# The low halves of the feed-forward output weights by an accumulating DMA instead of a subtraction on VectorE

## The chip, the cores and the metric

The kernel runs on one core of one Trainium2 chip. The metric is the device time of one execution in microseconds; the time before is the median of three runs, 1916.57 us (1915.85 to 1919.64). A profile of one further execution, taken by the hardware profiler, stands behind every row that is shown here.

## The reference

512 tokens of width 1024 go through two transformer blocks, all in float32. The first block has block-sparse attention and differential attention side by side, merged by gates, and a feed-forward; the second has a half-weighted feed-forward, two mixers, a cross attention to a memory and another half-weighted feed-forward. The three feed-forwards are alike, and the change lies in their last product alone:

```python
D_FF = -(-8 * D_MODEL // (3 * 256)) * 256          # 2816
f = (jax.nn.silu(h @ w_gate[l]) * (h @ w_up[l])) @ w_down[l]      # block 1

def swiglu(h, w_gu, w_down):                                      # block 2, twice
    gu = h @ w_gu
    gate, up = jnp.split(gu, 2, axis=-1)
    return (jax.nn.silu(gate) * up) @ w_down
```

## The kernel before

**Halves.** Every float32 operand of a large product is kept as two tiles of a shorter format (`F32R`): a high half, the rounded value, and a low half, the rest. One product is three matmuls (`mm3`: L371 high by high, L372 high weight or activation by the other's low, L373 low by high), summed in PSUM. The weights come as float32 from memory and are halved on the chip by `split` (L399 to L403): ScalarE copies the raw tile into the high half, which rounds it (L402), then VectorE subtracts the high half from the raw tile (L403).

**Weights' way.** `wpieces` streams a weight matrix in pieces of 128 x 1024 values (512 KB). SyncE issues one load for each (L263); two pieces share a raw slab `wr`, and there are two slabs. The halves go to tiles `wh` and `wl`, four buffers each. So a load waits until both pieces of the slab's last content have been halved, and a cast waits until TensorE has done with the `wh` that stood in its buffer four pieces earlier.

**Feed-forward.** The 22 k tiles of the inner width (2816 = 22 x 128) are done in groups: four k tiles each, the last one six. For a group TensorE makes the gate and up products (most of them by Winograd's seven products, for which VectorE also forms sums of the raw weights, L305 to L308), ScalarE the silu (L1264), VectorE the product of both (L1272), and `split` the halves `q` of the result. The output product of one group (`wide_steps` over `w_down`, L1286) is run in shares between the next group's gate and up products, by the generator `between`. It has two column parts of 512; a piece of `w_down` is two k tiles by 512 columns, so a feed-forward has 22 pieces of it, 16 within the loop and six behind it, of the last group. The last group's second part goes token tile by token tile (`by_token`), so that the norm that follows can begin with the first one. Only then are all its three pieces needed at once.

**Order.** Each engine runs its own instructions in the order that a scheduler gave them when the program was built; weights' loads and halvings have a higher priority (`WPRIO`). Engines wait for each other by semaphores. SyncE's queue carries all loads, among them `x_rows(x_d)` (L195), which in the last part of the first feed-forward brings back eight tiles of the residual stream that were spilled earlier to memory from GpSimd's queue (L554).

**Names.** In the rows below `b<-wh,q` is a `w_down` product of a weight's high half and an activation's half, `b<-wl,q` one with the low half; `a<-...` and `b<-w,...` are gate and up products. Buffers' numbers are left out in the profile, and stand behind the names in the order of instructions.

Of the kernel before, what the change touches and what calls it, by code (L numbers as in the profile page):

```python
# [14 lines left out]
AF = mybir.ActivationFunctionType  # L15
ALU = mybir.AluOpType
AX = mybir.AxisListType

P = 128
# [58 lines left out]
def STEP(pe=0.0, dve=0.0, act=0.0, ops=(), lat=0.0, free=0, need=0, back=0):  # L78
    """A part of a chain or of a product as weave sees it: time on the tensor engine; then on the vector engine and
    on the scalar engine, or on these and GpSimd (D, A, G) in turns; the least delay to the next part; banks freed and needed; how  # L80
    many parts back the next one's inputs lie."""
    return Step(pe, dve, act, ops, lat, free, need, back)
# [11 lines left out]
def transformer_blocks_kernel(  # L94
# [93 lines left out]
    def x_rows(src, get=None):  # L188
        """Token-major tiles: [t, u] holds tokens 128 t.. and columns 512 u.. ."""
        res = {}  # L190
        for t in range(4):
            for u in range(2):
                tl = (get or wt)()
                tc.keep_in_program_order(
                    nc.sync.dma_start(tl, src[t * P:(t + 1) * P, u * 512:(u + 1) * 512]))  # L195
                res[t, u] = tl
        return res
# [67 lines left out]

    def wslab(src, kt, cols, later=None):
        return list(wpieces(src, kt, cols, later))

    def wpieces(src, kt, cols, later=None):
        """Streams src ([kt*128, cols]) in pieces (k, n, high, low) of n k tiles from k on."""  # L270
        per = max(1, 1024 // cols)
        for k in range(0, kt, per):
            n = min(per, kt - k)
            if k % (2 * per) == 0:
                whole = raw_slab()
            raw = whole[:, k % (2 * per) * cols:][:, :n * cols]
            wload(raw, src, k, n, cols)
            hi, lo = [t[:, :n * cols] for t in halves_w()]
            halve = lambda hi=hi, lo=lo, raw=raw: split(hi, lo, raw)
            if later is None or k == 0:  # L280
                with tc.high_priority(WPRIO):
                    halve()
            else:
                later.append(halve)
            yield k, n, hi.rearrange("p (k c) -> p k c", c=cols), lo.rearrange("p (k c) -> p k c", c=cols)

    def sums_w(src):
        """Winograd's seven sums of a 256-column slab's quarters [k tile of a pair][half of the columns], in halves."""
# [23 lines left out]
    def sums_x(act, get):  # L312
        """The operand's side of it: per product the halves of its sum, pair of k tiles by pair."""
# [25 lines left out]
    def slab_sums(ws, xs):  # L339
        """A 256-column slab by Winograd's seven products: tiles of the first 256 tokens' first 128 columns and the others'  # L340
        second ones, and of the others' first and the first's second ones."""
# [33 lines left out]
    def slab_feat(slab, kt, act, bank=None):  # L375
        """Two 128-column outputs of a 256-column slab, features on partitions, one after the other."""
# [9 lines left out]
    def slab_tok(slab, kt, act, ntt, cols):  # L386
        """Token-major outputs of a slab, token tile by token tile."""
# [11 lines left out]
    def split(hi, lo, src, scale=None):  # L399
        """hi + lo = src * scale."""  # L400
# [14 lines left out]
    def in_order(chain):  # L415
        """Keeps what the blocks of one chain trace in this order on its engines."""
# [25 lines left out]
    def rms_col(sums, eps):  # L442
        """(sum of sums + eps) ** -0.5 per token."""
# [7 lines left out]
    def squares(f):  # L451
        """Per token the sum of squares over D."""
# [4 lines left out]
    class PreNorm:  # L457
        """Token-major rows -> feature-major operand: rows * rstd, transposed, times the gain, in halves."""
# [17 lines left out]
        def operand(self, src, *before):  # L476
            """The operand and, as its parts come, its product with the 256 columns of src; before that, other products."""
# [38 lines left out]
    class PostNorm:  # L516
        """x += rmsnorm(f) * g, by tokens, and on to the next norm."""
# [10 lines left out]
        def add(self, t, c0, f, fg, eng):  # L528
            """Takes columns c0.. of f; fg = f * gain."""
# [4 lines left out]
        def row(self, t):  # L534
            """In two stages, for others' work between them."""
# [36 lines left out]
    # distances s - t and the masks are kept negated: the logits are formed negated, so that their  # L572
    # minimum is at once the exponent's bias
# [19 lines left out]
    def stack_q(ps, scale, tag):  # L593
        """Of two heads' 64 features: per head [high; low], or the other way round, on 128 partitions."""
# [5 lines left out]
    def stack_k(ps, tag):  # L600
        """Of two heads' 64 features: per head [high; high] and [low; low] on 128 partitions."""
# [9 lines left out]
    def qk(ps, lh, rh):  # L611
        """All four terms of a head's product, one of its operands [high; low], the other twofold."""
# [5 lines left out]
    def softmax_rows(pt, bias, ps, su):  # L618
        """pt = exp(max - (bias + ps)) of the negated logits, su its row sums."""
# [23 lines left out]
    def fill_ready(accs, consume, dve, act, lat=0.0):  # L643
        """Products made with the norm."""
# [18 lines left out]
    def weave(chains, fills, width, banks, model):  # L663
        """Emits dependent chains, and independent products between their parts, as one order of the tensor engine.

        The parts of a chain that are not yet due, by what they cost each engine, leave room for a product.
        """
# [7 lines left out]
        def place(engine, t, d):  # L675
            """The end of d on an engine, in the first gap from t on."""
# [27 lines left out]
        def start(c):  # L704
            """When a chain's next part can start."""
# [42 lines left out]
    def flip(jobs):  # L748
        """Transposes [128 q, 128 keys] blocks side by side; returns their halves."""
# [43 lines left out]
    def p_flips(blocks, dst):  # L793
        """Transposed probability blocks [i, j], by key tiles: 0 with queries 0.., 1 with 128.., 2 and 3."""
# [20 lines left out]
    def fold(dst, ps, hh):  # L815
        """The two halves' sum on the head's partitions."""
# [4 lines left out]
    def moba_open(p_):  # L821
        """What the two heads of a pair share: the choice of blocks."""
# [78 lines left out]
    def diff_head(hd):  # L901
        """The first softmax is left unnormalised; its row sums come back with the norm."""
# [67 lines left out]
    # gated merge  # L970
# [108 lines left out]
    def mem_slabs(slabs):  # L1079
        """Products for the keys (0 - 3) and the values (4 - 7) of the memory's heads."""  # L1080
# [22 lines left out]
    def wide_steps(src, kt, act, emit, parts, early=True, begun=None, held=0):  # L1103
        """Token-major product: emit(tok tile, c0, psum) for the column parts (c0, cols, by_token).

        An emit in stages has the next token tile's first stage before its last. The first part may have been
        begun, with the first k tiles held in its accumulators.
        """
# [16 lines left out]
        for c0, cols, by_token in parts:  # L1125
            k0 = held if c0 == 0 else 0
            slab = ((k + k0, n, hi, lo) for k, n, hi, lo in wpieces(src[k0 * P:, c0:c0 + cols], kt - k0, cols))
# [86 lines left out]
    def pools(first, second, mid):  # L1214
        """Where the operand's sums lie, half of them in one place, and the middle's halves."""
# [3 lines left out]
    def ffn(wg, wu, wd, add, emit, groups, sums, rest, mid):  # L1219
        """sums: the slabs whose products take Winograd's form."""  # L1220
# [11 lines left out]
        def quarters(ts, wino, to_wino):  # L1232
            """Winograd's two tiles (wino) or those of 128 columns each: how the other form's, or the same, lie in them."""
# [6 lines left out]
        def by_tokens(pairs, wino):  # L1240
            """The two k tiles' halves, token tile by token tile."""
# [6 lines left out]
        for gi, (a, b) in enumerate(groups):  # L1248
# [3 lines left out]
            def between():  # L1252
                """A share of the last group's output product, between the slabs."""
# [32 lines left out]
            before = wide_steps(wd[a * P:b * P], n, mids, fn, ((0, 512, False), (512, 512, b == NF)), False)  # L1286
# [51 lines left out]
    def rstd_rows(sq, ones):  # L1338
        """(mean of squares of a token's head + 1e-6) ** -0.5, on every feature's partition."""
# [12 lines left out]
    def sigmoid(dst, src):  # L1352
        """exp(min(x, 0) - log(1 + exp(-|x|)))."""
# [6 lines left out]
    def hgrn_chain(hd):  # L1360
# [15 lines left out]
        def decayed(e, hl):  # L1376
            """e holds exponents; turned into key (lower) and query (upper) operands."""
# [22 lines left out]
        # the weights of key tile j with the queries from 128 j on, in halves  # L1400
# [113 lines left out]
    def sb_head(pair, hh):  # L1514
        """Stick-breaking attention, queries on partitions: with sp = log(1 + exp(z)) a key's weight is
        exp(z - the sum of sp from it to the last key before the query)."""
# [235 lines left out]
    def fill_mo():  # L1752
        """Half of the columns of the output product, as far as the first heads go; its accumulators stay open."""
# [75 lines left out]
```

## Time and profile before

| | |
|---|---|
| median of three runs | 1916.57 us |
| profiled execution, first to last instruction | 1918.7 us |
| TensorE's granted clock, mean | 0.995 of full speed |
| TensorE busy | 1885.0 us (98%) |
| VectorE busy | 1387.3 us (72%) |
| ScalarE busy | 929.8 us (48%) |
| GpSimd busy | 176.4 us (9%) |
| subtractions of weights' low halves, all weights | 381 of 1217 ns, 462.7 us |
| casts of weights' high halves, all weights | 381 of 1036 ns, 393.7 us |

The profile gives each engine's busy time over the span, cut into rows by line, engine, operation and tiles. A busy share is a mean over stages that differ, so the stages are cut out by windows in time. In a timeline each row is one instruction, or several alike in a row, with its start and duration; a bracket at its end tells how long the engine had been idle before it and what ended that. A chain of waits, followed back from the last instruction, tells which engine's work stood on the path that set the end.

### The profile page before, as it was taken

What the parts mean: (1) busy time and instruction counts of PE and PEld (TensorE: products, weight loads), DVE (VectorE), ACT (ScalarE), POOL (GpSimd) and SP (SyncE); (2) the same over time, 40 slices, a digit from 0 to 9 for tenths busy, and PEclk for the clock granted to TensorE, in tenths of its full rate; (3) what the DMA queues carried; (4) which work ended last, traced back from release to release, by engine and by line L of the source; (5) the groups of instructions that cost most, each with busy time, mean ns of one, the idle gap of its engine ahead of it and who ended that gap; (6) DMA issues with size and microseconds to landing.
All of it is one profiled execution on the core that took longest, in us unless ns stands there. A gap on an engine that the chain in (4) does not pass through costs nothing.

```text
span 1918.7 us, 29315 instructions
## 1 busy us (share of the span) xinstructions
PE 1885.0 (98%) x11566; PEld 1690.5 (88%) x11566; DVE 1387.3 (72%) x2217; ACT 929.8 (48%) x1537; POOL 176.4 (9%) x272
## 2 busy tenths in 40 slices
PE   8999999999999999999999999999999999999998
PEld 7899888888999998889999988888988778999997
DVE  6777635468778786677878757878886448878785
ACT  5666534364534345443344456657555344434443
POOL 2340100050000002000000010330420000000000
PEclk9999999999999999999999999999999999999999
DMA  5221223462232324423232342211223222332322
GB/s 180 67 67 56 78 66 132 143 203 88 89 111 90 122 91 163 150 88 111 88 111 88 110 159 88 66 45 39 90 93 110 77 75 84 106 110 89 111 88 88
DMA packets 161452, 192.40 MB, mean 100 GB/s; under 512 B 7361, under 2 KB 131362, under 8 KB 161314
## 3 DMA queue, kind: packets, MB, share of 16 engines
q1 hardware_dynamic: 159746, 185.80, 29.2%
q0 software_dynamic: 1280, 4.20, 0.6%
q8 instruction: 91, 1.49, 0.3%
q10 hardware_dynamic: 288, 0.52, 0.1%
q14 instruction: 47, 0.39, 0.1%
HBM read 182.11 MB, written 8.39 MB: 99 GB/s over the span
## 4 chain that ended last, share of the span: by engine, by line
PE 86%; issue 5%; DVE 4%; ACT 2%; POOL 1%; POOLq 0%; ACTq 0%; DVEq 0%
PE b L372 16%; PE b L373 16%; PE b L371 16%; PE a L371 10%; PE a L372 10%; PE a L373 10%; PE a L513 4%; PE b L615 1%; PE b L489 1%; DVE wl L403 1%; PE b L753 1%; PE b L1444 1%; DVE w L1540 1%; ACT wh L402 1%; PE b L883 0%
## 5 line engine op out<-in xcount | busy, mean ns | idle before, releaser
L403 DVE TENSOR_TENSOR wl<-wr,wh 128x1024 fp32r<-128x1024 f32 (+1 forms) x381 | 462.7, 1217 | 270.6 <-ACT wh L402 261.6
L402 ACT CAST wh<-wr 128x1024 fp32r<-128x1024 f32 (+1 forms) x381 | 393.7, 1036 | 439.0 <-PE b L372 152.3
L371 PE MATMUL b<-wh,q 128*128 128x512 f32 x672 | 262.4, 390 | 0.0
L372 PE MATMUL b<-wl,q 128*128 128x512 f32 x672 | 262.0, 390 | 0.0
L373 PE MATMUL b<-wh,q 128*128 128x512 f32 x664 | 258.5, 389 | 0.0
L371 PE MATMUL a<-h,wh 128*128 128x512 f32 (+1 forms) x660 | 238.2, 361 | 0.0
L373 PE MATMUL a<-h,wl 128*128 128x512 f32 (+1 forms) x660 | 234.9, 356 | 0.0
L372 PE MATMUL a<-h,wh 128*128 128x512 f32 (+1 forms) x660 | 234.7, 356 | 0.0
L372 PE MATMUL b<-h,wh 128*128 128x256 f32 (+1 forms) x568 | 175.9, 310 | 0.0
L371 PE MATMUL b<-h,wh 128*128 128x256 f32 (+1 forms) x568 | 175.9, 310 | 0.0
L373 PE MATMUL b<-h,wl 128*128 128x256 f32 (+1 forms) x568 | 175.9, 310 | 0.0
L371 PEld LDWEIGHTS b<-wh,q 128*128 128x128 f32 x672 | 126.3, 188 | 24.8
L373 PEld LDWEIGHTS b<-wh,q 128*128 128x128 f32 x664 | 124.7, 188 | 26.4
L372 PEld LDWEIGHTS b<-wl,q 128*128 128x128 f32 x672 | 126.3, 188 | 24.3
L372 PE MATMUL a<-s,wh 128*128 128x256 f32 (+1 forms) x488 | 141.2, 289 | 0.0
L373 PEld LDWEIGHTS a<-h,wl 128*128 128x128 f32 x660 | 124.6, 189 | 18.3
L371 PEld LDWEIGHTS a<-h,wh 128*128 128x128 f32 x660 | 124.7, 189 | 18.0 <-issue 0.5
L372 PEld LDWEIGHTS a<-h,wh 128*128 128x128 f32 x660 | 124.8, 189 | 17.9 <-issue 0.5
L372 PEld LDWEIGHTS b<-h,wh 128*128 128x128 f32 x568 | 108.3, 191 | 5.6
L373 PEld LDWEIGHTS b<-h,wl 128*128 128x128 f32 x568 | 108.2, 191 | 5.6
L371 PEld LDWEIGHTS b<-h,wh 128*128 128x128 f32 x568 | 108.1, 190 | 5.6
L372 PEld LDWEIGHTS a<-s,wh 128*128 128x128 f32 x488 | 93.1, 191 | 1.2
(374 smaller groups left out, 4201.9 us busy)
## 6 DMA issues: line engine op xcount, KB each, us to landing
wr<-in_ffn_w_gu_dram SPq DMA_DIRECT2D x88, 512.0 KB
wr<-in_w_in_dram SPq DMA_DIRECT2D x68, 512.0 KB
wr<-in_ffn_w_down_dram SPq DMA_DIRECT2D x44, 512.0 KB
wr<-in_w_gate_dram SPq DMA_DIRECT2D x22, 512.0 KB
wr<-in_w_up_dram SPq DMA_DIRECT2D x22, 512.0 KB
wr<-in_w_down_dram SPq DMA_DIRECT2D x22, 512.0 KB
wr<-in_mem_w_kv_dram SPq DMA_DIRECT2D x16, 512.0 KB
wr<-in_w_out_dram SPq DMA_DIRECT2D x10, 512.0 KB
```

The costliest lines, as they stand in the source:

```text
L371: T.matmul(ps, lh, rh, start=first, stop=False)
L372: T.matmul(ps, lh, rl, start=False, stop=False)
L373: T.matmul(ps, ll, rh, start=False, stop=last)
L402: A.copy(hi, src)
L403: V.tensor_tensor(lo, src, f32(hi), op=ALU.subtract)
L489: T.transpose(banks[k][:, t * P:(t + 1) * P], self.s[t, k // 4][:, (k % 4) * P:(k % 4 + 1) * P], ident)
L513: T.matmul(accs[m], lh, rh, start=c == 0 and n in (0, 2), stop=c == KT - 1 and n > 3)
L615: T.matmul(ps, lh[n], rh[n], start=n == 0, stop=n == 1)
L753: T.transpose(ps[:, o * P:(o + 1) * P], blk, ident)
L1444: T.matmul(ps[:, gg * 64:(gg + 1) * 64], e[:, gg * P:(gg + 1) * P], up, start=True, stop=True)
L1540: V.tensor_tensor_scan(out=back, data0=ones_c.to_broadcast([P, sl.stop - sl.start]), data1=back, initial=0.0, op0=ALU.mult, op1=ALU.add)
```

## The change

`wpieces` and `wide_steps` get a parameter `halver`, and the feed-forwards hand `split_added` to the output product's `wide_steps`. It makes the low half of a piece in another way: ScalarE writes the negated, rounded raw tile into the low half, and an accumulating DMA from GpSimd's queue adds the raw tile to it, from SBUF to SBUF. As the rounding of −x is minus the rounding of x, the sum is the same low half. All 66 pieces of `w_down` (22 in each of three feed-forwards) go this way; all other weights, among them the gate and up weights, stay with `split`. The rest of the diff blanks comments and docstrings, and moves line numbers by some lines.

```diff
+    def split_added(hi, lo, src):
+        A.copy(hi, src)
+        A.activation(lo, src, AF.Copy, scale=-1.0)
+        nc.gpsimd.dma_start(lo, src, accum_op=ALU.add)
...
-    def wpieces(src, kt, cols, later=None):
+    def wpieces(src, kt, cols, later=None, halver=None):
...
-            halve = lambda hi=hi, lo=lo, raw=raw: split(hi, lo, raw)
+            halve = lambda hi=hi, lo=lo, raw=raw: (halver or split)(hi, lo, raw)
...
-    def wide_steps(src, kt, act, emit, parts, early=True, begun=None, held=0):
+    def wide_steps(src, kt, act, emit, parts, early=True, begun=None, held=0, halver=None):
...
-            slab = ((k + k0, n, hi, lo) for k, n, hi, lo in wpieces(src[k0 * P:, c0:c0 + cols], kt - k0, cols))
+            slab = ((k + k0, n, hi, lo) for k, n, hi, lo in wpieces(src[k0 * P:, c0:c0 + cols], kt - k0, cols, None, halver))
...
-            before = wide_steps(wd[a * P:b * P], n, mids, fn, ((0, 512, False), (512, 512, b == NF)), False)
+            before = wide_steps(wd[a * P:b * P], n, mids, fn, ((0, 512, False), (512, 512, b == NF)), False,
+                                halver=split_added)
```

The scheduler gives a new order with it. In the order of instructions a row is one instruction with its line, its tiles and the semaphores that it waits for (`DMASW` those of transfers on GpSimd's queue, `DMAHW` those of SyncE's).

ScalarE at the end of the loop of block 2's first feed-forward; `wr_2027` is the slab of the last group's first two `w_down` pieces, `wr_2043` that of the first two pieces of its second part, `q` the halves that TensorE multiplies with them, L1264 the silu. Before:

```order
L402 CAST wh_2030_11163<-wr_2027_11132 128x1024 [waits DMAHW5_49,PE_49,Activation_49]
L1264 ACTIVATE w_1994_10900<-w_1994_10900 128x512 [waits DVE_49]
L1264 ACTIVATE w_1995_10901<-w_1995_10901 128x512 [waits DVE_49]
L402 CAST wh_2033_11193<-wr_2032_11191 128x1024 [waits DMAHW6_49,PE_49,Activation_49]
L402 CAST wh_2044_11243<-wr_2043_11241 128x1024 [waits DMAHW7_49,PE_49]
L402 CAST q_2018_11118<-w_2017_11116 128x512 [waits DVE_49]
L402 CAST q_2021_11124<-w_2020_11122 128x512 [waits DVE_49]
L402 CAST wh_2046_11248<-wr_2043_11241 128x1024 [waits DMAHW0_49,PE_49,Activation_49]
```

And after, from the same cast on:

```order
L268 CAST wh_2030_11202<-wr_2027_11170 128x1024 [waits DMAHW5_49,PE_49,Activation_49]
L269 ACTIVATE wl_2031_11203<-wr_2027_11170 128x1024 [waits DMASW5_49,PE_49]
L1270 ACTIVATE w_1995_10939<-w_1995_10939 128x512 [waits DVE_49]
L268 CAST wh_2033_11233<-wr_2032_11231 128x1024 [waits DMAHW6_49,PE_49,Activation_49]
L269 ACTIVATE wl_2034_11234<-wr_2032_11231 128x1024 [waits PE_49]
L268 CAST wh_2044_11284<-wr_2043_11282 128x1024 [waits DMAHW7_49,PE_49]
L269 ACTIVATE wl_2045_11285<-wr_2043_11282 128x1024 [waits PE_49]
L408 CAST q_2018_11156<-w_2017_11154 128x512 [waits DVE_49]
L408 CAST q_2021_11162<-w_2020_11160 128x512 [waits DVE_49]
L269 ACTIVATE wl_2047_11291<-wr_2043_11282 128x1024 [waits DMAHW0_49,DMASW6_49,PE_49]
```

Behind each cast stands a negation of the same raw tile (L269), two of them ahead of the two `q` casts; one silu now stands behind the cast and the negation of `wr_2027`'s second piece.

SyncE at the end of the first feed-forward; `wr_1440` and `wr_1445` are the slabs of the three pieces of the part that goes by tokens, `x_d` the spilled tiles. Before:

```order
L263 DMA wr_1440_7531<-in_w_down_dram 128x2x512 [waits DMAHW3_49,DMAHW2_49,DVE_49]
L263 DMA wr_1440_7531<-in_w_down_dram 128x2x512
L263 DMA wr_1445_7542<-in_w_down_dram 128x2x512 [waits DMAHW4_49,DVE_49]
L195 DMA w_1420_7492<-x_d_102 128x512 [waits DMASW0_49,PE_49,Pool_49]
L195 DMA w_1421_7494<-x_d_102 128x512 [waits DMASW5_49,PE_49]
```

And after (the last load's slab is called `wr_1445` in both, the numbers behind the names differ):

```order
L263 DMA wr_1440_7550<-in_w_down_dram 128x2x512 [waits DMAHW2_49,DMASW1_49,DMAHW3_49,DMASW0_49,Activation_49]
L263 DMA wr_1440_7550<-in_w_down_dram 128x2x512
L195 DMA w_1420_7511<-x_d_102 128x512 [waits PE_49,Pool_49]
L195 DMA w_1421_7513<-x_d_102 128x512 [waits PE_49]
L195 DMA w_1422_7515<-x_d_102 128x512 [waits PE_49]
L195 DMA w_1423_7517<-x_d_102 128x512 [waits DVE_49]
L195 DMA w_1424_7519<-x_d_102 128x512 [waits PE_49]
L195 DMA w_1425_7521<-x_d_102 128x512 [waits DMAHW4_49,PE_49]
L195 DMA w_1426_7523<-x_d_102 128x512 [waits DMAHW5_49,PE_49]
L195 DMA w_1427_7525<-x_d_102 128x512 [waits DMAHW6_49,PE_49]
L263 DMA wr_1445_7563<-in_w_down_dram 128x2x512 [waits DMAHW7_49,DMASW2_49,Activation_49]
```

The load of the last `w_down` piece has moved from ahead of the eight loads of `x_d` to behind them, and the loads into a slab that held `w_down` pieces now wait for transfers of GpSimd's queue (`DMASW`) and for ScalarE.

TensorE at the first `w_down` piece of the first feed-forward (`wh_1015`, `wl_1016`), in the middle of the first slab's gate and up products. Before:

```order
L372 MATMUL b_1007_4638<-s_968_4464,wh_1001_4630 128x256 [waits DVE_49]
L373 MATMUL b_1007_4638<-w_967_4463,wl_1002_4631 128x256
L371 MATMUL b_1010_4732<-wh_1015_4738,q_934_4367 128x512
L371 MATMUL b_1009_4640<-w_970_4470,bh_997_4619 128x256 [waits Activation_49]
L372 MATMUL b_1010_4732<-wl_1016_4739,q_934_4367 128x512
L373 MATMUL b_1010_4732<-wh_1015_4738,q_935_4368 128x512
L371 MATMUL a_1006_4637<-h_893_4167,wh_995_4615 128x256 [waits Activation_49]
```

And after:

```order
L379 MATMUL a_1008_4639<-w_962_4452,wl_1000_4625 128x256
L377 MATMUL a_1008_4639<-w_970_4470,wh_999_4624 128x256
L378 MATMUL a_1008_4639<-s_971_4471,wh_999_4624 128x256
L379 MATMUL a_1008_4639<-w_970_4470,wl_1000_4625 128x256
L377 MATMUL b_1010_4732<-wh_1015_4738,q_934_4367 128x512
L378 MATMUL b_1010_4732<-wl_1016_4739,q_934_4367 128x512 [waits DMASW0_49]
L379 MATMUL b_1010_4732<-wh_1015_4738,q_935_4368 128x512
L377 MATMUL b_1010_4732<-wh_1015_4738,q_938_4398 128x512
```

The piece's matmuls no longer stand among these products; they have moved 51 rows to the rear, and the first read of the low half waits for a transfer (`DMASW`).

## Rows read from the trace of the kernel before

**Rows 1.** the page's first part (busy, share, instructions) and the chain by engine
```profile
PE 1885.0 (98%) x11566; PEld 1690.5 (88%) x11566; DVE 1387.3 (72%) x2217; ACT 929.8 (48%) x1537; POOL 176.4 (9%) x272
...
PE 86%; issue 5%; DVE 4%; ACT 2%; POOL 1%; POOLq 0%; ACTq 0%; DVEq 0%
```

**Rows 2.** windows: the first feed-forward's loop; its end
```profile
core 0: us, PE busy (x) PEld busy (x) DVE busy (x) ACT busy (x) POOL busy (x), PEclk, DMA share, GB/s
470.00:710.00 240.00, 240.00 (x1688) 225.47 (x1688) 189.60 (x244) 102.23 (x133) 0.00 (x0) 1.00 0.32 106
...
729.00:736.00 7.00, 7.00 (x32) 5.81 (x31) 2.77 (x3) 1.05 (x1) 0.00 (x0) 1.00 0.94 333
```

**Rows 3.** timeline of TensorE (start, us, line, tiles)
```profile
458.39 0.39 PE L371 MATMUL b<-w,bh 128*128 128x256 f32 x1 [0.32 <-ACT w L402]
...
511.00 0.39 PE L372 MATMUL b<-wl,q 128*128 128x512 f32 x1
...
741.22 0.39 PE L372 MATMUL b<-wl,q 128*128 128x512 f32 x1
...
1105.74 0.39 PE L371 MATMUL b<-wh,q 128*128 128x512 f32 x1
...
1114.12 0.39 PE L372 MATMUL b<-wl,q 128*128 128x512 f32 x1
```

**Rows 4.** timeline of ScalarE, first feed-forward's loop
```profile
453.74 1.05 ACT L402 CAST wh<-wr 128x1024 fp32r<-128x1024 f32 x1 [1.35 <-PE b L372]
...
501.01 1.05 ACT L402 CAST wh<-wr 128x1024 fp32r<-128x1024 f32 x1 [0.20 <-PE b L373]
...
504.31 1.05 ACT L402 CAST wh<-wr 128x1024 fp32r<-128x1024 f32 x1 [1.53 <-DMA wr<-in_w_gate_dram]
```

**Rows 5.** timeline of VectorE, first feed-forward's loop
```profile
502.09 1.23 DVE L403 TENSOR_TENSOR wl<-wr,wh 128x1024 fp32r<-128x1024 f32 x1 [1.94 <-ACT wh L402]
```

**Rows 6.** costliest groups (busy us, mean ns, idle before and what ended it)
```profile
L403 DVE TENSOR_TENSOR wl<-wr,wh 128x1024 fp32r<-128x1024 f32 (+1 forms) x381 | 462.7, 1217 | 270.6 <-ACT wh L402 261.6
L402 ACT CAST wh<-wr 128x1024 fp32r<-128x1024 f32 (+1 forms) x381 | 393.7, 1036 | 439.0 <-PE b L372 152.3
```

**Rows 7.** timeline of ScalarE, ends of two feed-forwards
```profile
720.63 1.05 ACT L402 CAST wh<-wr 128x1024 fp32r<-128x1024 f32 x1 [3.61 <-PE b L372]
...
733.08 1.05 ACT L402 CAST wh<-wr 128x1024 fp32r<-128x1024 f32 x1 [4.39 <-PE b L373]
...
1084.19 2.00 ACT L402 CAST wh<-wr 128x1024 fp32r<-128x1024 f32 x2 [3.54 <-DVE wr L308]
...
1087.75 1.05 ACT L402 CAST wh<-wr 128x1024 fp32r<-128x1024 f32 x1 [0.99 <-PE b L372]
1088.70 1.15 ACT L1264 ACTIVATE w<-w 128x512 f32<-128x512 f32 x2
...
1099.24 1.23 ACT L402 CAST q<-w 128x512 fp32r<-128x512 f32 x2 [3.28 <-DVE w L1272]
...
1106.26 1.05 ACT L402 CAST wh<-wr 128x1024 fp32r<-128x1024 f32 x1 [4.67 <-PE b L373]
```

**Rows 8.** the tile x_d: its spills from GpSimd's queue
```profile
L554 POOL DMA_DIRECT2D x_d<-w x16: 542/548/809, 382.6 to 1129.8; - x16
...
DMA to landing us min/median/max: 2.3/4.2/6.7
```

**Rows 9.** timeline of SyncE's queue (issues; duration of a group of xN)
```profile
499.12 0.92 SPq L263 DMA_DIRECT2D wr<-in_w_gate_dram  x2
503.35 1.70 SPq L263 DMA_DIRECT2D wr<-in_w_down_dram  x2
513.55 0.92 SPq L263 DMA_DIRECT2D wr<-in_w_up_dram  x2
...
713.97 9.37 SPq L263 DMA_DIRECT2D wr<-in_w_down_dram  x4
723.44 3.96 SPq L195 DMA_DIRECT2D w<-x_d  x8
```

## The prediction

> **What bounds the kernel now.** I read the totals first: TensorE is busy for 1885.0 of the 1918.7 us, VectorE for 1387.3 [rows 1]. The chain that ended last is 86% TensorE and 4% VectorE [rows 1]. Then came the stretches in which the changed code runs, the three feed-forward loops. In the windows that I cut out of them TensorE is busy for all 240.00 of 240.00 us (the other two loops read the same) at the full clock (1.00, 2.4 GHz), while VectorE works 189.60 of 240 and ScalarE 102.23 [rows 2]. So VectorE, which loses work, is not late there; its 4% of the chain lies elsewhere. What counts is when a low half is ready against when TensorE asks for it. In the timelines a usual piece is cast at 501.01, subtracted from 502.09 to 503.32, and TensorE first reads its low half at 511.00 [rows 3 to 5]: 7.7 us in hand. 48 of the 66 pieces (16 in each feed-forward) lie in the loops like this; the other 18 stand at their ends, where ScalarE, SyncE and the slabs are in closer order.
>
> **What goes and what comes.** 66 subtractions of 1.217 us [rows 6] go: 80 us of VectorE. As it waits for casts and not TensorE for it, that gives 0. 66 negations come to ScalarE, which reads and writes the same tiles as the cast of 1.036 us [rows 6]; no row shows a scaled copy of this size, and I take 1.05 us (ends: 1.0, and 1.15, what the two silus of together the same size take [rows 7]). That is 69 us, or 17 in a 240 us window in which ScalarE has 138 idle: 0. And 66 accumulating transfers of 512 KB come to GpSimd's queue. GpSimd itself is busy for 0.00 us in the loops [rows 2], so each issues at once; before, one issue of its queue took 0.55 us (0.81 at most) [rows 8].
>
> **The price of one transfer, X,** from issue to landing, is the unknown. No row shows an accumulating transfer, or one from SBUF to SBUF. The nearest are the 16 spills to x_d, 256 KB each on the same queue: 2.3 us at the least, 4.2 in the middle, 6.7 at the most [rows 8]. A transfer of double the size takes between 2.3 and 13.4 us by them. I take 4.6, twice the shortest, as the shortest ran with the least beside it, and the loops' transfers occupy only 0.32 of the DMA engines [rows 2].
>
> The Trainium skill ("DMA: Bandwidth & Descriptors", Anatomy of one DMA — SWDGE (gpsimd) path) fits such a transfer as 2.0 us plus its bytes at 436 GB/s, an estimate of 3.2 us for 512 KB; with it the sum below would be about 1 us less. The shortest spill, 2.3 us for 256 KB [rows 8], is near that fit (2.6); the middle one is not.
>
> **The 48 pieces in the loops.** Cast ends 502.06, negation 503.1, so the transfer must land within 511.00 − 503.1 = 7.9 us. With X = 4.6 it lands at 507.7, 3.3 us early: 0. Two things also stand behind the landing. The raw slab is refilled only then: the load that began at 503.35, right behind the subtraction [rows 9], begins at 507.7. It has room: the next load on SyncE begins at 513.55 [rows 9], and TensorE reads the old slab's second piece only from 511.00, so that the new slab's first piece comes to ScalarE later than that. And ScalarE is 1.05 us longer before its next cast (504.31), which waited 1.53 us for a load anyway [rows 4]: 0.
>
> **The first piece of the first feed-forward** is moved behind 51 other matmuls, as the order of TensorE shows. That removes the 0.32 us in which TensorE's products stood waiting for a weight's cast on ScalarE [rows 3]: −0.3. Its cast starts at 453.74 [rows 4], the negation ends at 455.9, and 51 matmuls at 0.14 us (240 us over 1688, [rows 2]) put its use near 465: it has some 9 us.
>
> **The ends of the loops.** Here ScalarE gets two negations ahead of the casts that TensorE needs next, and a load waits for a transfer. In block 2's first feed-forward: two casts end at 1086.19 [rows 7], the first negation at 1087.2, a silu of 0.58 comes between, the cast of row 1087.75 moves to 1088.2 and its negation ends at 1090.3. At 1090.3 + 4.6 = 1094.9 the slab is free. A pair of loads and its first cast are 504.31 − 499.12 = 5.2 us apart [rows 4, 9]: 1100.1. Behind this cast and its negation (2.1 us), by ScalarE's new order, stand the two q casts (1.23, [rows 7]) and a subtraction of half size (0.6, [rows 6]): ready at 1104.1. TensorE wants them at 1105.74 [rows 3]: 1.6 us in hand, 0, and a stall of X − 6.2 in each of three ends otherwise. The last piece, read token by token, is cast at 1106.26 (it waits for TensorE to free its tile) and read at 1114.12 [rows 3, 7]: 7.86 − 2.1 = 5.8 us for X, 1.2 in hand: 0, and X − 5.8 in two ends otherwise.
>
> **The first feed-forward's last piece** is the exception. SyncE's order now has its load behind the eight loads of x_d, where before it ended the row of four at 723.34, ahead of them (723.44) [rows 9]. The slab is freed by the piece cast at 720.63 [rows 7]: + 2.1 + 4.6 = 727.3. The 2 MB of x_d need 6.3 us at the 333 GB/s of that stretch [rows 2] from 723.4: 729.7. Then come 512 KB more, 1.6 us, and 2 to 3 us of latency (the pair of loads above took 5.2 us, of which 1 MB at that rate is 3.1): landed 733 to 734.6. Before, its cast was at 733.08 and its use at 741.22 [rows 3, 7]. Now: cast to 734.6, negation to 736.7 with a square of the norm before it, + 4.6 = 741.3 to 742.7. I take **+1.5** (0 to 4).
>
> **The sum** at X = 4.6: −0.3 + 0 + 0 + 1.5 = +1.2 us. The profiled execution's span goes from 1918.7 to 1919.9; it lies 2.1 above the median of the three runs, 1916.57, so the median becomes **1917.8**. A difference under 0.2% (3.8 us) is one that a measurement of this kernel can't tell from none.
>
> **Rivals.**
> (a) *The slow accumulate*, on the other side of no change: each piece costs TensorE (X − 7.9) once X is over 7.9 us. For it: the addition reads its destination as well as its source, which no spill does, and it runs beside the weights' loads; the longest spill took 6.7 us for half the size [rows 8]. Against: no loop shows a transfer that is held up, the DMA engines being 0.68 idle [rows 2]. Price at X = 9.2 (the 4.6 all doubled): 48 × 1.3 + 3 × 3.0 + 2 × 3.4 + about 6 = +84, or about 2000 us; at 13.4 about +310.
> The Trainium skill ("Collectives: The Full Stack", The bandwidth ceiling) has an add in a transfer at half the rate of a copy, from 62.28 to 32.35 GB/s, as it needs two source reads. No row here shows an add; the rule speaks against this change if the 4.6 us are transfer and not latency.
> (b) *The middle*: X between 5.8 and 7.9. The loops hide it, the ends don't: 3 × (X − 6.2) + 2 × (X − 5.8) + 1.5 + (X − 4.6): +4 at 6.2, +14 at 7.9: 1920 to 1930. For it: the middle spill, doubled and less a fixed part, lies here.
> (c) *VectorE's relief counts*: at the three ends the q subtractions come sooner by 1.2 us, if these are late for TensorE by more than the row shows. 3 × 1.2 = −3.6, beside the −0.3: 1912.7. Against: by the rows they are not late: cast from 1099.24, ready at 1101.1, asked for at 1105.74 [rows 3, 7].
>
> **How the numbers follow.** Forecast (X under 6.2): 0.55, of which 0.50 falls within 0.2% (1912.7 to 1920.4) and 0.05 above, with the first end at its +4. (a) 0.20 and (b) 0.20, both slower. (c) 0.05, faster. So 0.05 faster, 0.50 same, 0.45 slower. The range goes from 1914.5 (no stall at any end, the 0.3, and half of (c)) to 1940, which holds all of (b) and the beginning of (a), X up to 8.0; most of (a) and half of (c) stay out, together 2 in 10.
>
> **What would show it.** Right: TensorE still busy for 240 of 240 us in the loops; VectorE near 1307 us in all, ScalarE near 999; the accumulating transfers landing in 3 to 6 us; one wait of 1 to 3 us at the first feed-forward's last piece, the read of row 741.22. Wrong: a wait of TensorE on a transfer's semaphore at each piece in the loops, which means X over 7.9; waits on the q casts at the three ends, (b); a whole run below 1912.7, (c); or loads that land later than 504.31's because the transfers crowd them, a step that I hold at nothing.

## The result and the profile after

The changed kernel takes 1935.89 us (median of four runs, 1934.96 to 1937.19) where the kernel before, now with four runs, takes 1917.99: a ratio of 1.0087, 95% interval 1.0072 to 1.0101. It is slower by some 18 us. The time lies within the stated range, above the forecast of 1917.8; the likeliest case, no difference, did not come. That it lies within the range is in part luck, as the last sections show. The profiled execution's span is 1935.5 us, 16.8 more than before.

The page of the changed kernel, first the busy times and the chain, as [rows 1]:

```profile
PE 1886.9 (97%) x11566; PEld 1689.3 (87%) x11566; DVE 1312.1 (68%) x2151; ACT 986.2 (51%) x1603; POOL 231.9 (12%) x338
...
PE 84%; issue 6%; DVE 3%; DMA 3%; ACT 3%; POOL 1%; POOLq 0%; ACTq 0%; SPq 0%; DVEq 0%
```

VectorE lost 75 us and ScalarE gained 56; neither is the reason for the time. New is the 3% that DMAs hold of the chain. The costliest groups tell who waited for one (busy and mean, then idle time ahead of the group and what ended it):

```profile
L378 PE MATMUL b<-wl,q 128*128 128x512 f32 x672 | 263.7, 392 | 12.3 <-DMA wl<-wr 12.3
...
L270 POOL DMA_DIRECT2D wl<-wr x66 | 57.0, 863 | 936.1 <-ACT wl L269 796.4
```

TensorE waited 12.3 us for landings of accumulating transfers. Windows show where not and where (columns as in [rows 2]): not in the loop, where TensorE is as full as before, but at the end of the first feed-forward, where it works 2.02 of 8 us and then gets a lower clock.

```profile
470.00:710.00 240.00, 240.00 (x1688) 225.46 (x1687) 171.33 (x228) 115.48 (x149) 12.90 (x15) 1.00 0.50 139
...
745.00:753.00 8.00, 2.02 (x6) 1.17 (x5) 1.23 (x1) 5.20 (x11) 0.86 (x1) 0.86 0.74 199
...
752.00:760.00 8.00, 7.88 (x23) 6.28 (x24) 2.32 (x4) 0.72 (x2) 1.81 (x2) 0.65 0.41 133
```

The five waits one by one, in TensorE's timeline (752.12 and 1128.93 are the reads of rows 741.22 and 1114.12 of [rows 3]):

```profile
738.46 0.39 PE L377 MATMUL b<-wh,q 128*128 128x512 f32 x1
740.92 0.50 PE L378 MATMUL b<-wl,q 128*128 128x512 f32 x1 [2.07 <-DMA wl<-wr]
741.26 0.39 PE L379 MATMUL b<-wh,q 128*128 128x512 f32 x1
...
744.21 0.50 PE L378 MATMUL b<-wl,q 128*128 128x512 f32 x1 [1.63 <-DMA wl<-wr]
...
752.12 0.79 PE L378 MATMUL b<-wl,q 128*128 128x512 f32 x1 [5.83 <-DMA wl<-wr]
752.71 0.63 PE L379 MATMUL b<-wh,q 128*128 128x512 f32 x1
...
1128.93 0.50 PE L378 MATMUL b<-wl,q 128*128 128x512 f32 x1 [1.02 <-DMA wl<-wr]
...
1914.24 0.50 PE L378 MATMUL b<-wl,q 128*128 128x512 f32 x1 [1.77 <-DMA wl<-wr]
```

All five are first reads of a piece that goes token by token: the three of the first feed-forward (9.5 us together; the expectations below have them as 2.2, 1.8 and 6.1, from one matmul's start to the next less the usual 0.23), and the last one of each of the other two. After the longest wait the matmuls take 0.63 to 0.79 us where 0.39 is usual: the clock has gone to its lower level (1.2 GHz). From 752 to 760 it was 0.65 of full on the mean, which costs 0.35 x 8 = 2.8 us.

So 12.3 us of waits and 2.8 of clock are 15.1, near the 16.8, but the ends cost more than that and another stage gives some back. The two traces run level up to the end of the first feed-forward (711.80 and 711.77 for the same matmul in its loop). The first `b<-s,wh` matmul behind it then starts 13.6 us later, of which its waits and the clock are 12.3:

```profile
754.60 0.28 PE L371 MATMUL b<-s,wh 128*128 128x256 f32 x1
```

```profile
768.19 0.28 PE L377 MATMUL b<-s,wh 128*128 128x256 f32 x1
```

A wait costs TensorE some 0.3 us more than its row says. A row's idle time begins at the end of the matmul before, but matmuls of 0.39 us usually start 0.23 apart (741.00, 741.22 and 741.45 in the trace before). From the start at 738.46 to that at 741.26 are 2.80 us, where two usual steps are 0.45, so 2.35 us are lost and not 2.07. Behind the end of block 2's first feed-forward TensorE also waits for ScalarE, which it did not before:

```profile
1149.86 2.57 PE L495 MATMUL b<-ident,y 128*128 128x128 f32 x20 [1.06 <-ACT w L1101]
```

What comes back lies in a stage that the change does not touch, where the granted clock was low for longer in the trace before than in the one after (columns as in [rows 2]):

```profile
1275.00:1285.00 10.00, 9.82 (x35) 7.67 (x36) 5.79 (x15) 5.19 (x13) 0.00 (x0) 0.66 0.26 90
```

```profile
1289.00:1299.00 10.00, 8.71 (x38) 7.04 (x39) 7.93 (x22) 5.64 (x16) 0.00 (x0) 0.83 0.32 105
```

By these windows that is 10 x 0.17 = 1.7 us; that it comes from the change is not shown. The mean clock of the whole execution is 0.995 in both traces.

How the first feed-forward's end came to this is seen on three queues. SyncE, against the last two lines of [rows 9]. In the trace before, the pair of loads into `wr_1440` went out at 717.30:

```profile
717.30 1.66 SPq L263 DMA_DIRECT2D wr<-in_w_down_dram  x2
```

After:

```profile
723.64 0.88 SPq L263 DMA_DIRECT2D wr<-in_w_down_dram  x2
...
724.62 7.97 SPq L195 DMA_DIRECT2D w<-x_d  x8
732.96 0.38 SPq L263 DMA_DIRECT2D wr<-in_w_down_dram  x1
```

The pair goes out 6.3 us later, since its slab is now free only when two transfers have landed. The chain that ended last has the later of the two and then the pair (start, duration):

```profile
717.32 6.19 DMA wl<-wr
723.64 6.33 DMA wr<-in_w_down_dram
```

So the pair runs into the 2 MB of x_d, and the last piece's load is issued behind these at 732.96. ScalarE's casts tell when the loads were there, and GpSimd's rows when the three transfers of these pieces were issued:

```profile
730.05 1.05 ACT L268 CAST wh<-wr 128x1024 fp32r<-128x1024 f32 x1 [7.44 <-DMA wr<-in_w_down_dram]
...
744.69 1.05 ACT L268 CAST wh<-wr 128x1024 fp32r<-128x1024 f32 x1 [9.71 <-DMA wr<-in_w_down_dram]
...
746.26 1.04 ACT L269 ACTIVATE wl<-wr 128x1024 fp32r<-128x1024 f32 x1
```

```profile
732.35 0.86 POOL L270 DMA_DIRECT2D wl<-wr  x1 [8.58 <-ACT wl L269]
734.34 0.86 POOL L270 DMA_DIRECT2D wl<-wr  x1 [1.13 <-ACT wl L269]
747.60 0.86 POOL L270 DMA_DIRECT2D wl<-wr  x1 [12.40 <-ACT wl L269]
```

The last load, 512 KB, took from 732.96 to 744.69, 11.7 us. Beside it ran the rest of x_d and the first two transfers, which took from 732.35 to TensorE's read at 740.92 (8.6 us) and from 734.34 to 744.21 (9.9 us). The third transfer, with less beside it, took 4.5 (747.60 to 752.12).

Last, the price X of all 66 transfers, from issue to landing, as [rows 8] for the spills (shortest, median, longest):

```profile
L270 POOL DMA_DIRECT2D wl<-wr x66: 852/862/944, 456.6 to 1909.0; - x66
...
DMA to landing us min/median/max: 4.5/4.9/9.8
```

### The profile page after: what moved, and what is told of

The parts are those of the page before. It is cut to its first block, busy times and chain, and to the rows that moved or that the text cites. A ratio compares the mean times of both kernels' runs of the same rounds, so it can differ in the third digit from the quotient of the medians.

```text
span 1935.5 us, 29501 instructions
## 1 busy us (share of the span) xinstructions
PE 1886.9 (97%) x11566; PEld 1689.3 (87%) x11566; DVE 1312.1 (68%) x2151; ACT 986.2 (51%) x1603; POOL 231.9 (12%) x338
## 4 chain that ended last, share of the span: by engine, by line
PE 84%; issue 6%; DVE 3%; DMA 3%; ACT 3%; POOL 1%; POOLq 0%; ACTq 0%; SPq 0%; DVEq 0%
PE b L378 14%; PE b L379 14%; PE b L377 14%; PE a L377 11%; PE a L378 11%; PE a L379 11%; PE a L519 4%; PE b L621 1%; DMA wl<-wr 1%; DMA wr<-in_w_down_dram 1%; PE b L495 1%; PE b L759 1%; PE b L1451 1%; DMA wr<-in_ffn_w_down_dram 1%; DVE wl L409 1%
## 5 line engine op out<-in xcount | busy, mean ns | idle before, releaser
L409 DVE TENSOR_TENSOR wl<-wr,wh 128x1024 fp32r<-128x1024 f32 (+1 forms) x315 | 382.9, 1219 | 325.7 <-ACT wh L408 324.3
L408 ACT CAST wh<-wr 128x1024 fp32r<-128x1024 f32 (+1 forms) x315 | 324.6, 1032 | 358.2 <-PE b L378 194.2
L378 PE MATMUL b<-wl,q 128*128 128x512 f32 x672 | 263.7, 392 | 12.3 <-DMA wl<-wr 12.3
L270 POOL DMA_DIRECT2D wl<-wr x66 | 57.0, 863 | 936.1 <-ACT wl L269 796.4
```

The source lines that it names most:

```text
L270: nc.gpsimd.dma_start(lo, src, accum_op=ALU.add)
L378: T.matmul(ps, lh, rl, start=False, stop=False)
L408: A.copy(hi, src)
L409: V.tensor_tensor(lo, src, f32(hi), op=ALU.subtract)
```

## The experiments

The theory after the result: the loops hide a transfer of 4.5 to 5 us, the ends do not, and at the first feed-forward's end loads and transfers meet on the same DMA engines and hold each other up. Rivals: the 66 negations on ScalarE; a loss that is spread over the loops; the place of the last load in SyncE's queue alone. Each experiment is an edit of the changed kernel; each ratio is against the kernel before on the same chip.

### The loops alone

```diff
-                                halver=split_added)
+                                halver=split_added if b < NF else None)
```

> Only the 16 pieces inside each feed-forward's loop (48 in all) get their low half by the accumulating transfer; the six of each last group are subtracted on VectorE as before. Theory (the loss of 18 us sits at the three ends, 13.5 us of it at the first feed-forward's, and the loops cost nothing): within 0.2% of before, 1914 to 1921 us, no wait of TensorE on a transfer's landing, X about 4.5 to 5.2 us. Rival (negations, or transfers that crowd the loads in the loops, cost time somewhere): 1925 us or more, with waits that show in the loops or at their ends.

Measured: 1920.65 us against 1919.81, ratio 1.0010 (1.0001 to 1.0020). 48 of the 66 transfers cost at most 0.2%. The view of the transfers' line names nobody who waited for one; its landing times and the window at the first feed-forward's end, where TensorE is full again:

```profile
DMA to landing us min/median/max: 4.5/4.6/6.7
```

```profile
710.00:755.00 45.00, 45.00 (x250) 39.36 (x250) 29.17 (x42) 19.11 (x34) 4.92 (x6) 1.00 0.43 141
```

### The ends alone

```diff
-                                halver=split_added)
+                                halver=split_added if b == NF else None)
```

> The mirror image: only the 18 pieces of the three last groups go by the accumulating transfer, the 48 in the loops are subtracted on VectorE. Theory (ends): 1932 to 1938 us, nearly the whole loss with 18 of 66 transfers, and the same stall of about 6 us at the last piece of the first feed-forward. Rival (loops or the sum of all): under 1926 us.

Measured: 1932.65 us, ratio 1.0064 (1.0047 to 1.0081): 12.8 us over before with 18 transfers, most of the full change's loss and perhaps all of it, as the intervals overlap. Their landing times and the wait for the last piece, which is even longer:

```profile
DMA to landing us min/median/max: 5.1/6.1/9.0
```

```profile
753.51 0.80 PE L378 MATMUL b<-wl,q 128*128 128x512 f32 x1 [7.17 <-DMA wl<-wr]
```

The same transfer that takes 4.6 us at the median in the loops takes 6.1 at the ends.

### The negations without the transfers

```diff
-        nc.gpsimd.dma_start(lo, src, accum_op=ALU.add)
+        V.tensor_tensor(lo, src, f32(lo), op=ALU.add)
```

> ScalarE still writes the negated rounded copy for all 66 pieces, but VectorE adds the raw tile to it instead of the transfer, so the 66 negations are alone in the time. Theory (transfers and what waits for their landing are the loss): 1915 to 1921 us. Rival (ScalarE's 69 us of negations ahead of the casts that TensorE needs are the loss): 1925 us or more, with waits on casts at the three ends.

Measured: 1919.47 us, ratio 1.0001 (0.9991 to 1.0012). ScalarE's 66 further instructions cost nothing, at the ends too: the rival of the negations falls. In the window of the loop ScalarE has its additional work and TensorE no gap:

```profile
470.00:710.00 240.00, 240.00 (x1687) 225.37 (x1687) 189.82 (x244) 113.93 (x148) 0.00 (x0) 1.00 0.32 106
```

### The loads of x_d moved behind

```diff
-        if not xt:
+        if u == 1 and not xt:
             xt.update(x_rows(x_d))
```

> All 66 transfers stay, but the eight loads of the spilled residual x_d in the first feed-forward are asked for later, so that on SyncE's queue they stand behind the load of the last w_down piece (and behind the four loads of the memory's weights, which have moved ahead of them too). Theory of the order (the last piece's load stands behind 2 MB of x_d): that load lands at about 733 to 736 instead of 744.6, the stall of 6.1 us before the last piece falls to 0 to 2 us, and the time to 1922 to 1930 us, unless x_d itself is now late for the norm that follows. Rival theory (the transfers that run beside it slow this load, wherever it stands): it lands later than 738 and the stall stays above 4 us, time 1932 us or more.

Measured: 1923.81 us, ratio 1.0022 (1.0013 to 1.0032): 14 of 18 us are back with all 66 transfers in place. SyncE now issues the last piece's load right behind the three before it and x_d at 744.12, and of the waits at the first feed-forward's end one of 0.92 us is left:

```profile
714.50 15.45 SPq L263 DMA_DIRECT2D wr<-in_w_down_dram  x4
740.65 3.43 SPq L263 DMA_DIRECT2D wr<-in_mem_w_kv_dram  x4
744.12 6.51 SPq L195 DMA_DIRECT2D w<-x_d  x8
```

```profile
743.15 0.50 PE L378 MATMUL b<-wl,q 128*128 128x512 f32 x1 [0.92 <-DMA wl<-wr]
```

So the loss needs x_d between the last loads. It does not say yet whether the place in the queue or the traffic on the engines did it, as the edit changes both.

### The pieces read token by token subtracted again

```diff
-            slab = ((k + k0, n, hi, lo) for k, n, hi, lo in wpieces(src[k0 * P:, c0:c0 + cols], kt - k0, cols, None, halver))
+            slab = ((k + k0, n, hi, lo) for k, n, hi, lo in wpieces(src[k0 * P:, c0:c0 + cols], kt - k0, cols, None, None if by_token else halver))
```

> Of the 66 pieces, the nine that are read token by token (three at each end) are subtracted on VectorE again; the other 57 keep the accumulating transfer. SyncE's order in the first feed-forward still has the last piece's load behind the eight loads of x_d. Theory (order and shared DMA engines together: the load is slow because two transfers run beside it, and the transfers are slow because the loads run beside them): the last piece's load, with no transfer of these pieces beside it, lands at 736 to 740 instead of 744.6, the three stalls of 2.2, 1.8 and 6.1 us in the first feed-forward's end fall to under 2 us together, those of 1 to 2 us at the other two ends vanish; 1919 to 1925 us. Rival (the place behind x_d on the queue alone makes the load late): it lands after 742, a stall of 3 us or more stays, 1927 us or more.

Measured: 1920.11 us, ratio 0.9998 (0.9988 to 1.0007): 57 transfers are free, nine cost the 18 us. The last piece's load still stands behind the eight loads of x_d. The pair is as late as in the changed kernel (722.68). But no transfer runs beside the last load now, and it takes from 730.71 to ScalarE's cast at 737.66, 7.0 us, where it had taken 11.7:

```profile
722.68 1.62 SPq L263 DMA_DIRECT2D wr<-in_w_down_dram  x2
...
724.39 5.94 SPq L195 DMA_DIRECT2D w<-x_d  x8
730.71 0.38 SPq L263 DMA_DIRECT2D wr<-in_w_down_dram  x1
```

```profile
737.66 1.05 ACT L408 CAST wh<-wr 128x1024 fp32r<-128x1024 f32 x1 [5.95 <-DMA wr<-in_w_down_dram]
```

The rival of the queue's order alone falls: with the same order the load came within the 736 to 740 us of the theory. Order and company make the loss together, and removing either removes most of it. This edit also takes the transfers' own 4.5 to 9.8 us out of the way of these pieces; how the loss divides between the later load and the longer transfers, no run tells. That all DMA engines are shared by whoever issues is also what the Trainium skill says ("DMA: Bandwidth & Descriptors", Issuing engines are not separate DMA queues); the 11.7 against 7.0 us agree with it.

### The first feed-forward subtracted again

```diff
-                                halver=split_added)
+                                halver=None if sums is FFN1[1] else split_added)
```

> The first feed-forward's 22 pieces are subtracted on VectorE as before; the 44 of the other two keep the accumulating transfer. Theory (13.5 us of the loss sit at the first feed-forward's end, where x_d is loaded): 1919 to 1925 us, with stalls of 1 to 2 us at the two other ends. Rival (each feed-forward loses a like share): about 1930 us.

Measured: 1923.59 us, ratio 1.0025 (1.0013 to 1.0036). The first feed-forward's share of the 0.87% is thus some 0.62%, 12 us. The other two lose 2.5 to 7 us by the interval; of that the trace shows two waits for transfers, 0.7 us and this one of 0.8 at the last end, and one of 0.8 for ScalarE behind the end of block 2's first feed-forward. The rest of it is not placed:

```profile
1897.66 0.50 PE L378 MATMUL b<-wl,q 128*128 128x512 f32 x1 [0.82 <-DMA wl<-wr]
```

```profile
PE b L495 <- ACT w L1101: 0.8, 1, 0.8
```

### A copy in place of the addition

```diff
-        nc.gpsimd.dma_start(lo, src, accum_op=ALU.add)
+        nc.gpsimd.dma_start(lo, src)
```

> Each of the 66 transfers copies the raw tile over the low half instead of adding it; all else, sizes, queue and order, stays, so that only the addition's own price is taken away (the low halves are then the whole weights and the result is another). Theory (the addition reads its destination too, and so moves at half a copy's rate): a lone transfer in the loops lands in 3.2 to 3.7 us instead of 4.5. Rival (the price is latency, and an addition costs no more than a copy): 4.3 to 4.6 us. The time falls by some us against the full change, to 1922 to 1933, if the ends lose by the transfers' length.

Measured: 1924.81 us in one run, 5.8 above the kernel before. Issue and landing of the 66 copies, to be read beside 852/862/944 and 4.5/4.9/9.8:

```profile
L270 POOL DMA_DIRECT2D wl<-wr x66: 530/530/617, 456.3 to 1894.5; - x66
...
DMA to landing us min/median/max: 2.9/3.2/8.1
```

The addition costs 1.6 us over a copy of the same bytes (4.5 − 2.9, shortest against shortest); 0.33 us of that is the longer issue on GpSimd, as the time to landing counts from the issue's start. The shortest copy lies below the expected 3.2 to 3.7, the median at its lower end, and the rival of 4.3 to 4.6 falls. The long end stays (8.1): a copy beside the loads is slow too. Of TensorE's five waits for transfers one is left (us in total, times, longest), so in this run shorter transfers alone take most of the loss away:

```profile
PE b L378 <- DMA wl<-wr: 3.2, 1, 3.2
```

The Trainium skill's fit ("DMA: Bandwidth & Descriptors", Anatomy of one DMA — SWDGE (gpsimd) path), 2.0 us and the bytes at 436 GB/s, gives an estimate of 3.2 us for the copy; the shortest took 2.9, the median 3.2. With the data's part doubled, as the Trainium skill has it for an addition with two source reads ("Collectives: The Full Stack", The bandwidth ceiling), the estimate is 2.0 + 2.4 = 4.4; the shortest addition took 4.5, the median 4.9. Both agree within half a microsecond; the addition's price over a copy, 1.6 us, is above the 1.2 of these estimates.

### Twice the transfer

The kernel in which the pieces by token are subtracted again, with each of its 57 transfers issued twice in a row.

```diff
         nc.gpsimd.dma_start(lo, src, accum_op=ALU.add)
+        nc.gpsimd.dma_start(lo, src, accum_op=ALU.add)
```

> As e7_tokens_plain, but each of the 57 transfers is issued twice, the second behind the landing of the first, so that the raw tile is added twice (the low halves then hold a whole weight too much and the result is another). It doubles X alone, to some 9.0 to 9.6 us (two of 4.5 and a gap). Theory (the loops hide 7.9 us and no more, as the subtraction's end and the first read of the low half showed): each of the 48 pieces in the loops now stalls TensorE by 1 to 1.7 us, 45 to 80 us in all, time 1965 to 2000 us. Rival (the casts run ahead by more than that, and the loops would hide a slower transfer as well): under 1930 us.

Measured: 2005.85 us in one run against 1918.91: +87, a little over the 45 to 80 that were expected. Who waited for the second transfers (us, times):

```profile
PEld b L379: 72.2, 51
PE b L379: 56.0, 51
```

51 waits of 1.1 us, for 57 doubled transfers. The mean clock of the run was 0.986 where it was 0.995, which is 18 us of 2004, so that waits and clock make 74 of the 87. The other 13 are near what each wait costs beside its row, some 0.3 us, 51 times. The rival, a deeper cover, falls: what the loops hide ends between one transfer and two.

## Why the prediction was right and where it was wrong

**Right.** X in the loops was taken as 4.6 us from the shortest spill, and is 4.6 at the median there (4.5 to 6.7 with the loops alone). The budget of 7.9 us per piece holds: one transfer leaves TensorE at 240 of 240 us, two in a row stall it nearly every time. That VectorE's relief is worth nothing, that the negations are free (they add 56 us to ScalarE's busy time, where 69 were reckoned, and cost 0.0001 ± 0.001 of the whole) and that the first piece's wait of 0.32 us goes away came out too. Rival (a), the slow accumulate, did not come: an addition costs 1.6 us over a copy, and the 4.6 us do not double. That it is the data's part alone that doubles fits the estimates above, but no run measured two sizes. Of rival (c), a gain at the three ends, nothing showed.

**Wrong: one X for all places.** The steps for the three ends used the loops' 4.6 us. At the ends transfers come close together beside a burst of loads, and most take 5 to 9.8 us.

**Wrong: the last piece at block 2's two ends.** The stall there was to be X − 5.8. It was 1.02 and 1.77 us, and X − 5.8 gives neither: these two transfers took 6.5 us (1122.46 to the read at 1128.93) and 5.2 (1909.04 to 1914.24), so 0.7 and nothing.

```profile
1122.46 0.86 POOL L270 DMA_DIRECT2D wl<-wr  x1 [1.04 <-ACT wl L269]
...
1909.04 0.86 POOL L270 DMA_DIRECT2D wl<-wr  x1 [4.29 <-ACT wl L269]
```

The term that failed with it is the 5.8 us. The step let ScalarE wait only for TensorE to free a tile. Now it stands waiting for the loads of these pieces, into slabs that are free only at a landing, and the last transfer is issued late:

```profile
1116.27 1.05 ACT L268 CAST wh<-wr 128x1024 fp32r<-128x1024 f32 x1 [7.15 <-DMA wr<-in_ffn_w_down_dram]
...
1907.68 1.07 ACT L269 ACTIVATE wl<-wr 128x1024 fp32r<-128x1024 f32 x1 [3.15 <-DMA wr<-in_ffn_w_down_dram]
```

**Wrong: the first feed-forward's last piece, +1.5 us.** It waited 5.83, with a lower clock after it. The step let x_d start at 723.4 and the last load land by 734.6; the load was there at 744.69. What it left out stands in the prediction itself, in the step on the other ends: there a pair of loads waits for the transfers of its slab. The same pair, here 1 MB into `wr_1440`, was moved from 717.30 to 723.64, in front of x_d, and the two transfers that follow it fell in the middle of that burst. I counted 2 MB and 512 KB on the engines; 1 MB of loads and 1 MB of transfers were there too.

**Wrong: two waits that no step had.** The first two pieces by token of the first feed-forward cost 2.07 and 1.63 us. I had reckoned the first feed-forward's end like block 2's, where no x_d is loaded.

**Held at nothing, and decisive:** "loads that land later than 504.31's because the transfers crowd them" stood among the signs of being wrong, with no price. In the loops it cost nothing. At the first feed-forward's end it made the last load 4.7 us longer (11.7 against 7.0), and the loads the transfers.

**Rival (b)** gave 1920 to 1930 us and was nearest in time, but not by its mechanism: it had one slow X that stalls three ends alike, by waits for the `q` casts. The loss is some 12 us at one end and a few at the others, with X unchanged elsewhere. The range held 1935.89 only because its upper part was left for (a)'s beginning, a stall at each piece in the loops. None came, so that the time fell into that part is luck.

No version beats the kernel before. The loops alone, all but the pieces by token, and the negations with a VectorE addition are the same within 0.2%: an engine that TensorE does not wait for gives nothing back when it loses work.

## What to carry to other kernels

A transfer has no price of its own: take it lone for steady loops, and where it meets a burst, add up all bytes that are on the DMA engines in that stretch, those that the change itself moves there included. When work is moved from an engine to a transfer, ask at each buffer what now waits for the landing, and follow the loads that this delays to the next burst in their queue. In a kernel whose TensorE is full, a pipeline's end, where three pieces are needed at once, decides; try the change in the steady part and at the end separately before anything else.

## What the runs showed of the hardware

An accumulating transfer of 512 KB from SBUF to SBUF on GpSimd's queue took 4.5 us at the least, a copy of the same tile 2.9; the issue on GpSimd took 0.86 us against 0.53. Beside a burst of loads the addition took up to 9.8 us and the copy 8.1, and a load of 512 KB beside two additions 11.7 us against 7.0 with none. Around a wait of 5.83 us, with 2.02 us of work in 8 us, TensorE's granted clock fell to its lower level, and was 0.65 on the mean over the next 8 us.
